# A net of two blocks on one core: subtractions of the fp32r split moved from GpSimd to VectorE, seven casts from VectorE to ScalarE

## The chip, the core and the metric

The kernel runs on one core of one Trainium2 chip, as one launch. The metric is the device time of that launch in microseconds (us). The engines are named as the profile names them: PE (TensorE matmuls), PEld (its weight loads), DVE (VectorE), ACT (ScalarE), POOL (GpSimd) and SP (SyncE, which issues the DMAs).

## What is computed

The reference is a chain of residual layers on 256 tokens of width 1024: a first block of two layers (banded attention with a short convolution, then a gated feed-forward of width 2816) and a second block of two layers (an mLSTM mixer or a stick-breaking mixer, and after it a PEER feed-forward). Cut to the part that the change's largest piece lies in:

```python
def peer_ffn(h, w_q, sub_keys, peer_u, peer_v):
    ...
        s_top, i_top = lax.top_k(s, PEER_TOPK)
    ...
        g_top, pos = lax.top_k(cand, PEER_TOPK)
        expert = jnp.take_along_axis(cand_idx, pos, axis=-1)
        g = jax.nn.softmax(g_top, axis=-1)
        u = jnp.take(peer_u, expert, axis=0)
        act = jax.nn.gelu(jnp.einsum('thkd,td->thk', u, xb).astype(jnp.float32), approximate=False)
        vv = jnp.take(peer_v, expert, axis=0)
        return jnp.einsum('thk,thkd->td', (g * act).astype(xb.dtype), vv)
```

Every sublayer is `x = x + g * norm_or_gate(f(norm(x)))`, so that the next sublayer's first product needs the norm of the whole new row of x.

## The kernel before, in words

The 256 tokens are two tiles of 128 rows (t = 0 and 1). Every weight is streamed from HBM once, as tiles of 128x1024 f32 (`load`, L166, issued by SP). `split_w` makes two fp32r tiles of each: `whi`, a cast (L177, as a rule on ACT), and `wlo` = raw - whi (L180, on DVE or POOL). Activations are split the same way, and `mm3` makes each product as three fp32r matmuls: high by high, high by low, low by high (L185 to L187). Four raw tiles, five `whi` and five `wlo` are held at a time.

**Which engine splits.** A counter `ahead` is set to 0 in `Norm.finish` each time the second row tile's norm is set up. The first four tiles of a stage after that take their engines from two strings (L29): the casts from `FIRST_HI` = "aava" (a is ACT, v is DVE), the subtractions from `FIRST_LO` = "vpvp" (v is DVE, p is POOL). Later tiles are cast on ACT and subtracted on DVE, unless the caller names an engine. The fifth and sixth tile's casts are held behind the norm.

**A transition** is the place between two stages. When the last matmuls of a stage are done, row tile t = 0 is finished first: on DVE the scaled result is made (L300, or L567), x updated (L305, or L568), the sums of squares (ACT, L74) turned into `rstd` (ACT L260, DVE L261), and x times rstd is written to `f` or `xa` by a pair of TENSOR_SCALAR (L91). PE transposes it (`tpx`, L96), ACT and DVE split the transposes into `hhi` and `hlo` (L102 to L106), and the first product of the new stage (`mmA`) can start. The first four weight tiles are split in the same time, on the same engines. There are seven such transitions whose tiles follow the strings; in the first stage of all there is no earlier work to wait for.

**The PEER layers** (`peer`) hold the rest of what the change touches; there are two. For 128 groups of experts, `up(c)` makes a product with 24 matmuls and a gelu. Groups 0 to 63 run beside the routing (top-16 searches on DVE, subtractions on POOL for every third c). After it, for c from 64 to 99, `up` runs beside 32 calls of `weigh`: masks (`e`, L958, L959, L964, on DVE), 16 small matmuls (`pG`, L968) and a multiplication of the activations by the weights (L976, DVE); subtraction on POOL for c % 6 == 1. Then 28 turns of `down(c)` and `up(100 + c)`; then, for c from 28 to 63, `down(c)` with the other 32 calls of `weigh` (below: the weighing stretch); then `down` alone up to 127. `down(c)` casts the activations (`wr`, L988, ACT), subtracts (`wr`, L989: POOL for 28 <= c < 64, else DVE), splits a weight tile (POOL for c % 6 == 1 and c < 64, else DVE) and adds 12 matmuls of 512 columns into four accumulators `acc`.

The program is built by a layer that lists each engine's instructions in the order of a plan, and each engine then runs its list in that order. When an instruction is given to another engine, the lists of all engines can come out in another order.

The lines that the change touches:

```python
29    FIRST_HI, FIRST_LO = "aava", "vpvp"
177   (nc.vector.tensor_copy if FIRST_HI[i:i + 1] == "v" else nc.scalar.copy)(hi, raw)
179   lo_eng = nc.gpsimd if FIRST_LO[i:i + 1] == "p" else nc.vector
180   self.last_lo = lo_eng.tensor_tensor(lo, raw, hi.bitcast(F32), op=ALU.subtract)
```

Of the kernel before, what the change touches and what calls it, by code (L numbers as in the profile page):

```python
# [7 lines left out]
F32 = mybir.dt.float32  # L8
# [5 lines left out]
ALU = mybir.AluOpType  # L14
# [11 lines left out]

WSCALE = 32768.0

FIRST_HI, FIRST_LO = "aava", "vpvp"  # L29

FREE, LAST = 4, 6

# [83 lines left out]
class Net:  # L116
# [776 lines left out]
    def peer(self, l, norm, g2, nxt, out=None):  # L893
        nc, tc, d = self.nc, self.tc, self.d


        N1, NA, FIN, GATE, TAIL = 64, 100, 58, 110, 4
        LAG = 128 - NA
        with ExitStack() as ctx:
# [11 lines left out]
            def up(c, dst, lo_eng=None):  # L911
                w = self.split_w(d["peer_u"][l, c], lo_eng=lo_eng)
                p = self.pa.tile([128, S], F32, tag="sc", name="pA")
                for k in range(KD):
                    mm = self.mm3(p, [v[:, k * 128:(k + 1) * 128] for v in w], [v[:, k, :] for v in h],
                                  k == 0, k == KD - 1)
                return mm, nc.scalar.activation(dst, p, AF.Gelu)  # L917

            def spare(full=False):
                self.calls += 1  # L920
                if self.bg and (self.calls % 2 or full):
                    self.pop()
# [24 lines left out]
            def row(c):  # L947
                c = c % NA
                return act1[:, c, :] if c < N1 else act2[:, c - N1, :]
# [30 lines left out]
            def down(c):  # L980
                if not acc:
                    acc.extend([self.ps.tile([128, 512], F32, tag="mm", name="acc") for _ in range(2)] for _ in range(NT))
                if c < 128 - TAIL // 2:
                    gh, gl = wr[:, 0, c % 2, :], wr[:, 1, c % 2, :]
                else:
                    w2 = C.tile([128, 2, S], F32R, tag="wr2", name="wr2")
                    gh, gl = w2[:, 0], w2[:, 1]
                nc.scalar.copy(gh, row(c))  # L988
                (nc.gpsimd if LAG <= c < 64 else nc.vector).tensor_tensor(gl, row(c), gh.bitcast(F32), op=ALU.subtract)  # L989
                v = self.split_w(d["peer_v"][l, c], lo_eng=nc.gpsimd if c % 6 == 1 and c < 64 else nc.vector)  # L990

                def mm(t, j):
                    ts_ = slice(t * 128, (t + 1) * 128)
                    self.mm3(acc[t][j], (gh[:, ts_], gl[:, ts_]), [y[:, j * 512:(j + 1) * 512] for y in v],
                             c == 0, c == 127)

                if c >= 128 - TAIL:
                    return mm
                for t in range(NT):
                    for j in range(2):  # L1000
                        mm(t, j)

            done = 0
            for c in range(64, NA):
                up(c, row(c), nc.gpsimd if c % 6 == 1 else nc.vector)
                while done < 32 and done * (NA - 65) < (c - 63) * 32:
                    weigh(0, 8 * done)
                    done += 1
            for c in range(LAG):
                down(c)  # L1010
                up(NA + c, row(NA + c), nc.gpsimd if c == 0 else nc.vector)
                spare(True)
            done = 0
            for c in range(LAG, 64):
                down(c)
                while done < 32 and done * (63 - LAG) < (c - LAG + 1) * 32:
                    weigh(1, 8 * done)
                    done += 1
            for c in range(64, 128 - TAIL):
                down(c)  # L1020
                spare(2 * len(self.bg) > GATE - c)
                if c == NA - 1:
                    mid.close()
                    C = P(ctx, "pec", 2)
                if c == GATE:
                    tc.keep_in_program_order(nc.scalar.preload_act_table_set("sqrt_and_others"))
                    if nxt:
                        nxt.prepare()
                    gb = [C.tile([128, 512], F32, tag="g2b", name="g2b") for _ in range(2)]
                    for j in range(2):  # L1030
                        nc.sync.dma_start(gb[j], g2()[:, j * 512:(j + 1) * 512])
# [305 lines left out]
```

## Time and profile before

| | before |
|---|---|
| median of 3 runs (lowest to highest) | 2943.63 us (2941.0 to 2946.9) |
| the profiled execution | 2948.3 us, span 2946.5 us |
| PE, PEld | 2892.2 us (98%), 2600.3 us (88%) |
| DVE | 2176.6 us (74%) |
| ACT | 1424.7 us (48%) |
| POOL | 339.8 us (12%), 176 instructions |
| granted PE clock, mean | 0.987 |
| L180 on DVE, on POOL | 799 and 94 instructions |
| L989 on DVE, on POOL | 184 and 72 instructions |
| L177 on ACT, on DVE | 886 and 7 instructions |

The profile is one execution, 4.7 us above the median of the runs (2948.3 - 2943.63). Its span lies 1.8 us inside its time (2948.3 - 2946.5). An engine's busy share is a mean over stages that have different limits; what a stage is worth is read in the stage. A start in a row is counted from the start of the span; the number in square brackets is how long the engine sat idle before the instruction, and what released it. The granted clock is a share of the full 2.4 GHz.

### The profile page before, as it was taken

What the parts mean: (1) busy time and instruction counts of PE and PEld (TensorE: products, weight loads), DVE (VectorE), ACT (ScalarE), POOL (GpSimd) and SP (SyncE); (2) the same over time, 40 slices, a digit from 0 to 9 for tenths busy, and PEclk for the clock granted to TensorE, in tenths of its full rate; (3) what the DMA queues carried; (4) which work ended last, traced back from release to release, by engine and by line L of the source; (5) the groups of instructions that cost most, each with busy time, mean ns of one, the idle gap of its engine ahead of it and who ended that gap; (6) DMA issues with size and microseconds to landing.
All of it is one profiled execution on the core that took longest, in us unless ns stands there. A gap on an engine that the chain in (4) does not pass through costs nothing.

```text
span 2946.5 us, 50678 instructions
## 1 busy us (share of the span) xinstructions
PE 2892.2 (98%) x19693; PEld 2600.3 (88%) x19693; DVE 2176.6 (74%) x4064; ACT 1424.7 (48%) x2356; POOL 339.8 (12%) x176
## 2 busy tenths in 40 slices
PE   9999999999999999989999999999999999999999
PEld 7898997899897779989999887877899999988887
DVE  6886766886755576978876897686689787459765
ACT  6645445554544554444344334556544434443454
POOL 0001001000100002330100330010023210014100
PEclk9999999999999899999999999999999999999999
DMA  6385775366665444564478458754345545654564
GB/s 220 108 282 185 265 244 184 104 236 231 215 195 171 132 143 152 178 201 145 155 269 281 153 158 276 224 175 129 122 159 180 179 137 158 186 179 139 165 201 146
DMA packets 153572, 542.41 MB, mean 184 GB/s; under 512 B 20003, under 2 KB 21227, under 8 KB 153331
## 3 DMA queue, kind: packets, MB, share of 16 engines
q1 hardware_dynamic: 153330, 539.18, 56.9%
q8 instruction: 154, 2.52, 0.3%
q14 instruction: 88, 0.71, 0.1%
HBM read 538.02 MB, written 1.09 MB: 183 GB/s over the span
## 4 chain that ended last, share of the span: by engine, by line
PE 88%; DVE 10%; DMA 1%; ACT 1%; issue 1%; POOL 0%; SPq 0%; DVEq 0%; ACTq 0%; POOLq 0%
PE acc L185 8%; PE acc L187 8%; PE acc L186 8%; PE mmB L186 7%; PE mmB L187 7%; PE mmB L185 7%; PE pA L185 6%; PE pA L186 6%; PE pA L187 6%; PE mmA L185 5%; PE mmA L186 5%; PE mmA L187 5%; PE pG L968 4%; DVE wlo L180 3%; PE sc L185 1%; DVE whi L177 1%
## 5 line engine op out<-in xcount | busy, mean ns | idle before, releaser
L177 ACT CAST whi<-raw 128x1024 fp32r<-128x1024 f32 x886 | 929.6, 1050 | 822.0 <-PE pA L186 313.7
L180 DVE TENSOR_TENSOR wlo<-raw,whi 128x1024 fp32r<-128x1024 f32 x799 | 988.8, 1241 | 340.8 <-ACT whi L177 337.7
L185 PE MATMUL pA<-hhi,whi 128*128 128x256 f32 x2048 | 586.5, 286 | 10.8 <-ACT act L917 9.8
L186 PE MATMUL pA<-hlo,whi 128*128 128x256 f32 x2048 | 579.9, 283 | 0.0
L187 PE MATMUL pA<-hhi,wlo 128*128 128x256 f32 x2048 | 579.6, 283 | 0.0
L180 POOL TENSOR_TENSOR wlo<-raw,whi 128x1024 fp32r<-128x1024 f32 x94 | 252.6, 2687 | 2143.1 <-ACT whi L177 1897.9
L186 PE MATMUL mmB<-hlo,whi 128*128 128x256 f32 x1480 | 423.2, 286 | 0.0
L187 PE MATMUL mmB<-hhi,wlo 128*128 128x256 f32 x1480 | 421.6, 285 | 0.0
L185 PE MATMUL mmB<-hhi,whi 128*128 128x256 f32 x1480 | 421.5, 285 | 0.0
L185 PEld LDWEIGHTS pA<-hhi,whi 128*128 128x128 f32 x2048 | 394.3, 193 | 15.0 <-ACT act L917 11.4
L185 PE MATMUL acc<-whi,wr 128*128 128x512 f32 x1024 | 405.7, 396 | 0.0
L187 PE MATMUL acc<-whi,wr 128*128 128x512 f32 x1024 | 400.2, 391 | 0.4
L186 PE MATMUL acc<-wlo,wr 128*128 128x512 f32 x1024 | 399.4, 390 | 0.0
L186 PEld LDWEIGHTS pA<-hlo,whi 128*128 128x128 f32 x2048 | 393.2, 192 | 2.2
L187 PEld LDWEIGHTS pA<-hhi,wlo 128*128 128x128 f32 x2048 | 393.0, 192 | 0.0
L988 ACT CAST wr<-act 128x256 fp32r<-128x256 f32 x256 | 103.7, 407 | 405.9 <-PE acc L186 401.0
L186 PEld LDWEIGHTS mmB<-hlo,whi 128*128 128x128 f32 x1480 | 282.9, 191 | 4.3
L187 PEld LDWEIGHTS mmB<-hhi,wlo 128*128 128x128 f32 x1480 | 282.9, 191 | 2.3
L185 PEld LDWEIGHTS mmB<-hhi,whi 128*128 128x128 f32 x1480 | 282.9, 191 | 1.5
L187 PEld LDWEIGHTS acc<-whi,wr 128*128 128x128 f32 x1024 | 192.2, 188 | 45.8 <-DVE wr L989 4.7
L185 PEld LDWEIGHTS acc<-whi,wr 128*128 128x128 f32 x1024 | 193.9, 189 | 35.8
L186 PEld LDWEIGHTS acc<-wlo,wr 128*128 128x128 f32 x1024 | 192.8, 188 | 36.1
(359 smaller groups left out, 4238.2 us busy)
## 6 DMA issues: line engine op xcount, KB each, us to landing
raw<-in_peer_u SPq DMA_DIRECT2D x256, 512.0 KB, 3.7
raw<-in_peer_v SPq DMA_DIRECT2D x256, 512.0 KB, 4.2
adaw<-in_ada_w SPq DMA_DIRECT2D x96, 512.0 KB, 4.6
raw<-in_w_gates SPq DMA_DIRECT2D x80, 512.0 KB, 3.7
raw<-in_w_down SPq DMA_DIRECT2D x44, 512.0 KB, 4.3
raw<-in_w_gate SPq DMA_DIRECT2D x36, 512.0 KB, 4.2
raw<-in_w_up SPq DMA_DIRECT2D x36, 512.0 KB, 3.8
raw<-in_w_qkv SPq DMA_DIRECT2D x24, 512.0 KB, 4.4
```

What stands on the lines that cost most here:

```text
L177: (nc.vector.tensor_copy if FIRST_HI[i:i + 1] == "v" else nc.scalar.copy)(hi, raw)
L180: self.last_lo = lo_eng.tensor_tensor(lo, raw, hi.bitcast(F32), op=ALU.subtract)
L185: nc.tensor.matmul(out, lhsT=lhs[0], rhs=rhs[0], start=start, stop=False)
L186: nc.tensor.matmul(out, lhsT=lhs[0], rhs=rhs[1], start=False, stop=False)
L187: return nc.tensor.matmul(out, lhsT=lhs[1], rhs=rhs[0], start=False, stop=stop)
L968: nc.tensor.matmul(pg[:, :, 4 * g + t], lhsT=e2[:, g, :, t], rhs=e1[:, j, :, t], start=(j == 0), stop=(j == 1))
L988: nc.scalar.copy(gh, row(c))
```

## The change

```diff
-FIRST_HI, FIRST_LO = "aava", "vpvp"
+FIRST_HI, FIRST_LO = "aaaa", "vvvv"
...
                 nc.scalar.copy(gh, row(c))
-                (nc.gpsimd if LAG <= c < 64 else nc.vector).tensor_tensor(gl, row(c), gh.bitcast(F32), op=ALU.subtract)
-                v = self.split_w(d["peer_v"][l, c], lo_eng=nc.gpsimd if c % 6 == 1 and c < 64 else nc.vector)
+                nc.vector.tensor_tensor(gl, row(c), gh.bitcast(F32), op=ALU.subtract)
+                v = self.split_w(d["peer_v"][l, c], lo_eng=nc.vector)
...
             for c in range(64, NA):
-                up(c, row(c), nc.gpsimd if c % 6 == 1 else nc.vector)
+                up(c, row(c), nc.vector)
...
-                up(NA + c, row(NA + c), nc.gpsimd if c == 0 else nc.vector)
+                up(NA + c, row(NA + c), nc.vector)
```

Seven casts go from DVE to ACT. Fifty subtractions of a weight tile go from POOL to DVE: 14 at the seven transitions, and 36 in the two PEER layers (12 in `up` for c from 64 to 99, 2 in `up(100)`, 22 in `down`). All 72 subtractions of activations on POOL go to DVE. The routing's 44 subtractions (c < 64, c % 3 == 0) stay on POOL, with four multiplications and two memsets.

The first place is the first transition that uses the strings, on DVE. `rstd_3279` scales the last result of the old stage, `x_89` is row tile 0 and `x_97` row tile 1, `rstd_3293` is the norm of tile 0.

```order
 L305 SCALAR_TENSOR_TENSOR x_89<-f,rstd_3279,x_89 128x512 x2
-L177 CAST whi<-raw 128x1024
+L180 TENSOR_TENSOR wlo<-raw,whi 128x1024
 L76 TENSOR_SCALAR ss<-ss 128x1
-L180 TENSOR_TENSOR wlo<-raw,whi 128x1024
+L180 TENSOR_TENSOR wlo<-raw,whi 128x1024 x2
 L261 RECIPROCAL rstd_3293<-rstd_3293 128x1
+L300 TENSOR_TENSOR f<-mmA,gb 128x512
 L91 TENSOR_SCALAR f<-x_89,rstd_3293 128x512 x2
-L300 TENSOR_TENSOR f<-mmA,gb 128x512
```

Between the update of x and the norm's pair L91, DVE had a cast and one subtraction; now it has three subtractions and the second row tile's L300.

The second place is the same transition on ACT, where `junk` is the square of x that gives the sum of squares.

```order
 L260 ACTIVATE rstd_3279<-ss_3142 128x1
 L177 CAST whi<-raw 128x1024
-L74 ACTIVATE junk,ss<-x_89 128x512 x2
+L74 ACTIVATE junk,ss<-x_89 128x512
+L177 CAST whi<-raw 128x1024
+L74 ACTIVATE junk,ss<-x_89 128x512
+L177 CAST whi<-raw 128x1024
 L260 ACTIVATE rstd_3293<-ss 128x1
-L177 CAST whi<-raw 128x1024
```

Two casts now stand ahead of the `rstd` of tile 0, one of which was on DVE and one behind it.

The third place is the weighing stretch of the first PEER layer, on DVE. A tile `pG_n` is one call of `weigh`; the product with `wlo_19053` stands right behind the matmuls of `pG_19021` in PE's list, before and after. The first fence is one turn before.

```order
L180 TENSOR_TENSOR wlo_19194<-raw_19191,whi_19193 128x1024 [waits DMAHW7_49,Activation_49]
L976 SCALAR_TENSOR_TENSOR act2_14791<-pG_19021,act2_14791 128x36x8 [waits PE_49]
L976 SCALAR_TENSOR_TENSOR act1_11731<-pG_19021,act1_11731 128x28x8
L964 TENSOR_TENSOR e1_19073<-e0_19070,slots_11727 128x512
L964 TENSOR_TENSOR e1_19083<-e0_19070,slots_11727 128x512
L958 TENSOR_TENSOR e2_19116<-iota4_106,slots_11727 128x1024
L959 TENSOR_TENSOR e0_19164<-iota4_106,slots_11727 128x512 [waits DVE_49]
```

The second is the same turn of the change.

```order
L964 TENSOR_TENSOR e1_19026<-e0_19023,slots_11727 128x512 [waits DVE_49]
L964 TENSOR_TENSOR e1_19036<-e0_19023,slots_11727 128x512
L180 TENSOR_TENSOR wlo_19053<-raw_19050,whi_19052 128x1024 [waits DMAHW4_49]
L976 SCALAR_TENSOR_TENSOR act2_14791<-pG_19021,act2_14791 128x36x8 [waits PE_49]
L976 SCALAR_TENSOR_TENSOR act1_11731<-pG_19021,act1_11731 128x28x8
L958 TENSOR_TENSOR e2_19069<-iota4_106,slots_11727 128x1024
L959 TENSOR_TENSOR e0_19070<-iota4_106,slots_11727 128x512
L989 TENSOR_TENSOR wr_11723<-act1_11731,wr_11723 128x256 [waits Activation_49]
```

Beside the multiplication of `pG_19021`, DVE made the `wlo` that PE needs three turns later; now it makes there the one that PE needs next. The masks `e0` were also made a turn further ahead. The subtraction L989 is new in this list.

## Rows read from the trace of the kernel before

**Rows 1.** The page: engines, the chain that ended last, two groups (busy us, mean ns).

```profile
PE 2892.2 (98%) x19693; PEld 2600.3 (88%) x19693; DVE 2176.6 (74%) x4064; ACT 1424.7 (48%) x2356; POOL 339.8 (12%) x176
...
PE 88%; DVE 10%; DMA 1%; ACT 1%; issue 1%; POOL 0%; SPq 0%; DVEq 0%; ACTq 0%; POOLq 0%
...
L177 ACT CAST whi<-raw 128x1024 fp32r<-128x1024 f32 x886 | 929.6, 1050 | 822.0 <-PE pA L186 313.7
...
L180 POOL TENSOR_TENSOR wlo<-raw,whi 128x1024 fp32r<-128x1024 f32 x94 | 252.6, 2687 | 2143.1 <-ACT whi L177 1897.9
```

**Rows 2.** What PE waited for, whole span: us in total, times, longest us.

```profile
PE tpx L96 <- DVE f L91: 12.2, 6, 2.2
PE tpx L96 <- DVE xa L91: 11.2, 4, 3.9
```

**Rows 3.** Timeline of the first transition, DVE: start us, us, instruction [idle before].

```profile
270.52 2.89 DVE L177 CAST whi<-raw 128x1024 fp32r<-128x1024 f32 x1
...
273.45 1.23 DVE L180 TENSOR_TENSOR wlo<-raw,whi 128x1024 fp32r<-128x1024 f32 x1
...
274.78 2.97 DVE L91 TENSOR_SCALAR f<-x,rstd 128x512 f32<-128x512 f32 x2
277.68 0.68 DVE L300 TENSOR_TENSOR f<-mmA,gb 128x512 f32<-128x512 f32 x1
```

**Rows 4.** The same timeline, POOL.

```profile
270.15 2.71 POOL L180 TENSOR_TENSOR wlo<-raw,whi 128x1024 fp32r<-128x1024 f32 x1 [222.10 <-ACT whi L177]
274.88 2.60 POOL L180 TENSOR_TENSOR wlo<-raw,whi 128x1024 fp32r<-128x1024 f32 x1 [2.02 <-ACT whi L177]
```

**Rows 5.** The same timeline, ACT.

```profile
273.57 0.29 ACT L260 ACTIVATE rstd<-ss 128x1 f32<-128x1 f32 x1 [2.12 <-DVE ss L76]
```

**Rows 6.** The same timeline, PE.

```profile
272.78 0.40 PE L187 MATMUL mmA<-whi,mixlo 128*128 128x512 f32 x1
275.32 0.65 PE L96 MATMUL tpx<-ident,f 128*128 128x128 f32 x4 [2.15 <-DVE f L91]
277.81 0.88 PE L96 MATMUL tpx<-ident,f 128*128 128x128 f32 x4 [1.83 <-DVE f L91]
278.73 0.80 PE L185 MATMUL mmA<-whi,hhi 128*128 128x512 f32 x1
```

**Rows 7.** Timeline of DVE at the second transition, the second row tile's pair.

```profile
479.83 0.88 DVE L91 TENSOR_SCALAR f<-x,rstd 128x512 f32<-128x512 f32 x2
```

**Rows 8.** Windows of 14 us at the seven transitions: busy by engine, PEclk, DMA share, GB/s.

```profile
1945.00:1959.00 14.00, 8.29 (x29) 5.97 (x28) 13.91 (x23) 5.50 (x13) 7.22 (x4) 0.70 0.50 145
2086.00:2100.00 14.00, 10.62 (x51) 8.16 (x51) 13.76 (x26) 7.71 (x20) 4.83 (x2) 1.00 0.40 123
sum 98.00, PE 69.37 PEld 52.06 DVE 93.12 ACT 53.97 POOL 38.17; mean PE 9.91 PEld 7.44 DVE 13.30 ACT 7.71 POOL 5.45
```

**Rows 9.** A window over the weighing stretch of the first PEER layer, same columns.

```profile
1624.00:1780.00 156.00, 155.24 (x1066) 128.53 (x1066) 137.22 (x238) 60.19 (x89) 50.12 (x42) 1.00 0.52 164
```

**Rows 10.** Timeline of the weighing stretch, POOL.

```profile
1643.44 1.03 POOL L989 TENSOR_TENSOR wr<-act,wr 128x256 fp32r<-128x256 f32 x1 [2.93 <-ACT wr L988]
1647.24 0.98 POOL L989 TENSOR_TENSOR wr<-act,wr 128x256 fp32r<-128x256 f32 x1 [2.77 <-ACT wr L988]
...
1652.02 2.41 POOL L180 TENSOR_TENSOR wlo<-raw,whi 128x1024 fp32r<-128x1024 f32 x1
1654.86 0.79 POOL L989 TENSOR_TENSOR wr<-act,wr 128x256 fp32r<-128x256 f32 x1 [0.43 <-ACT wr L988]
1659.07 1.81 POOL L989 TENSOR_TENSOR wr<-act,wr 128x256 fp32r<-128x256 f32 x1 [3.42 <-ACT wr L988]
```

**Rows 11.** Groups of DVE from 1624.5 to 1780 us: count, busy us, mean ns.

```profile
L180 DVE TENSOR_TENSOR wlo<-raw,whi 128x1024 fp32r<-128x1024 f32 x38 | 46.2, 1217 | 8.6 <-ACT whi L177 8.6
L964 DVE TENSOR_TENSOR e<-e,slots 128x512 f16<-128x512 f16 x62 | 36.8, 617 | 1.5 <-PE pG L968 1.1
...
L989 DVE TENSOR_TENSOR wr<-act,wr 128x256 fp32r<-128x256 f32 x6 | 2.5, 421 | 1.6 <-ACT wr L988 1.6
```

**Rows 12.** All of line 964, by form: duration ns min/median/max.

```profile
L964 DVE TENSOR_TENSOR e<-e,slots x256: 403/417/2286, 1331.4 to 2759.2; 128x512 f16<-128x512 f16 x128
```

## The prediction, made before the change was run

> **What bounds the kernel now.** I read the page first, then what PE waited for, then one transition on four engines, then the weighing stretch. PE is busy for 98% of the span and carries 88% of the chain that ended last; DVE carries 10% and POOL 0% [rows 1]. So POOL's own length costs nothing as a sum (the 94 weight subtractions there take 252.6 us, 2.69 us each), and a change that gives DVE more work can gain only where the chain runs through DVE. What PE waited for says where that is: its transposes waited 12.2 us for `f` and 11.2 us for `xa`, both line 91, in ten waits [rows 2]. PE's idle time is there too: the seven windows of 14 us around the transitions hold 98 us, of which PE was busy 69.4, so 28.6 us are idle [rows 8].
>
> The first transition shows why line 91 is late. The pair of TENSOR_SCALAR takes 2.97 us [rows 3], and the same pair takes 0.88 us where POOL has nothing to do [rows 7]. POOL's subtraction started 0.10 us after it and ran 2.60 us [rows 4]; the long part of the pair has the length of that subtraction. The cast on DVE repeats it: 2.89 us from 270.52, beside a POOL subtraction that ran from 270.15 to 272.86. So these two DVE instructions stood still while POOL's subtraction ran, some 2 us each, both in the chain between the update of x and the first transpose. The chain ends with the pair at 277.75, the second four transposes at 277.81 and the first product at 278.73, while the last product of the old stage started at 272.78 [rows 6].
>
> **The transitions, step by step.** The change removes the DVE cast and both POOL subtractions and adds two DVE subtractions, and it puts L300 ahead of the pair. DVE then has, from 270.52 on: three subtractions of 1.23 [rows 3], the two tiny ss and rstd steps (0.15 each, my round figure for what is left between the rows), L300 at 0.68 and the pair at 0.88: 3.69 + 0.30 + 0.68 + 0.88 = 5.55, ending at 276.07 if nothing holds it. ACT is what may hold it. It gets two casts of 1.05 us [rows 1] ahead of its `rstd`, but sat idle for 2.12 us before that [rows 5]: 271.45 + 2.10 = 273.55, which is where its rstd started anyway. The third subtraction cannot start before that cast ends: 273.55 + 1.23 + 0.15 + 0.68 + 0.88 = 276.49. Against 277.75 the pair ends 1.26 to 1.68 us earlier. I take 1.5 for each of the seven, which have the same order of work: **-10.5 us**. The ends: nothing, if the casts wait for tiles that the old stage still reads, or if `hlo` becomes the late one (both updates of the second row tile now stand ahead of it on DVE); and 2.97 - 0.88 = 2.09 for each, -14.6 us in all, if everything that stood still is saved.
>
> The seven casts cost ACT 7 x 1.05 = 7.4 us of an engine that is busy for 48% of the span [rows 1]; beside the idle time just named I count them at nothing. SP's order of loads is not touched.
>
> **Outside the weighing stretch.** In `up` for c from 64 to 99 and in the turns of `down` with `up`, the moved subtractions (14) go onto a DVE that runs beside 24 matmuls of PE for each; a subtraction on DVE costs 1.2, but each on POOL held up a mask L964, which takes 0.42 us at the median and 2.29 at most [rows 12]. That is 1.87 saved against 1.22 spent; I count nothing. If DVE were the bound there, the 14 would cost at most 14 x 1.22 = 17 us, but the chain's 88% of PE speaks against it.
>
> **The weighing stretch** is where the change can lose. One turn takes 3.80 us (wr starts at 1643.44 and 1647.24 [rows 10]), and PE is busy for 155.24 of 156 us [rows 9]. Where a POOL subtraction stands in it, the turn from 1654.86 to 1659.07 takes 4.21, so it lost 0.41; there are three such turns in the first stretch and as many in the second. They go: 6 x 0.4 = **-2.4 us**.
>
> Against that, DVE gets more to do. In the first stretch it was busy for 137.2 us [rows 9]. The 62 masks L964 fall from 36.8 us to 62 x 0.417 = 25.9 [rows 11, 12], since POOL no longer holds them up: -10.9. Six subtractions come, 6 x 1.217 = +7.3, and 36 of the activations at 0.421 = +15.2 [rows 11]. That makes 148.8 of 156, or 95% (it was 88%). DVE's own work still fits, but its order has no lead left: in the second half of the list, some 19 turns, the `wlo` made in a turn is the one that PE needs next, where it was one for three turns later, and the multiplication L976 behind it waits for PE. With no lead every short wait of DVE for PE is handed back to PE. No row shows such a turn. The price is at least 0, because the sum of the work fits, and at most the 0.41 us of the turns in which DVE was late, in all 2 x 36 turns: 29.5 us. I take a third of 0.41, 0.13, for the 19 turns of either layer, nearer to the low end since 7.2 us of a stretch stay free: 2 x 19 x 0.13 = **+5 us**.
>
> The Trainium skill (Perfetto Trace Analysis, Optimizing Scalar/DVE Operations) speaks against the change here: where VectorE is saturated, it says, offloading some work to ScalarE or even GpSimd may make sense. By that sentence the weighing stretch should have kept its subtractions on POOL, and the sum would go with the high end of this term, some 15 us above the time before. The same section adds that GpSimd and VectorE share an SBUF read port, so that moving work between the two might not help; the 2.97 us against 0.88 agree with that.
>
> **Sum.** -10.5 - 2.4 + 5 = -7.9 on the profiled execution's 2948.3: 2940.4 us. That execution is 4.7 above the median of the runs shown, so on the scale of the median 2943.63 - 7.9 = 2935.7; I give **2936**. A measurement of this kernel can tell about 0.2% from no change, 5.9 us, so faster means below 2937.7 and slower above 2949.5.
>
> **The rivals.**
>
> *The gain is half eaten.* ACT's casts or `hlo` come late, so that a transition gains 0.8 instead of 1.5 (-5.6), or the weighing turns cost 0.25 instead of 0.13 (+9.5). Either gives about -3: 2940. For it: the ACT path above leaves no spare time at all (273.55 against 273.57). Against it: a cast late by 0.5 us would move only one subtraction.
>
> *VectorE becomes the bound of the weighing stretch: slower.* DVE has 7.2 us free in a stretch of 36 turns (156 - 148.8), 0.2 us a turn. If its waits for PE take more than that in a turn, each turn is longer than PE's 3.80, and the mechanism decides there. The whole price, 0.41 in all 72 turns, is 29.5, less the 10.5 of the transitions: +19, or 2963; it is slower than before by over 5.9 us from 0.23 us a turn on (10.5 + 5.9 = 16.4, over 72). For it: the missing lead, and L976 right behind `wlo`. Against it: the 88% of before held PE at 99.5% busy, and what held the masks up goes away.
>
> *The clock stays up: faster still.* The windows show a granted clock of 0.70 at the sixth transition and 1.00 at the seventh, where PE was busy for 10.62 us against 9.91 in the mean [rows 8]. 0.70 is a mix of the two levels, 1.2 and 2.4 GHz. The first product after the gap took 0.80 us at the first transition, twice the 0.40 before it [rows 6]. If shorter gaps keep the clock up at half of the seven, each gives back at most 0.30 x 14 = 4.2 us; with about 2 each, -7 more: 2929. Against it: a gap of 4.5 us is still a gap.
>
> *The change does not do what it says.* The order of the lists shows that it does; no chance.
>
> **Chances.** The forecast 0.45, half eaten 0.35, VectorE the bound 0.15, clock 0.05. So faster 0.50 (forecast and clock), same 0.35, slower 0.15. The range goes from 2927 (all of 2.09 us saved at each transition, no price in the weighing stretch: -17, or 2926.6) to 2950, where the slower rival begins with 0.23 us a turn; most of that rival and the luckiest clocks are left out. Where the signs meet, the likeliest case alone runs from 2931 to 2938.
>
> **What would show it.** Right: the pair L91 takes 0.9 us at all seven transitions, POOL shows only 44 weight subtractions, PE's waits for `f` and `xa` fall from 23.4 us to about 13, L964 has no instance above 0.5 us in the weighing stretch, and a turn there takes 3.80 in its first half and about 3.9 in its second. Wrong: PE waits for `hlo` or `wlo` at the transitions as long as it did for L91; or the turns of the weighing stretch go above 4.0 us, with PE waiting for L964 or for `wlo` in each.

## The result, and the profile after

| | before | after |
|---|---|---|
| median (lowest to highest), 5 runs each | 2943.63 us (2941.0 to 2948.44) | 2926.9 us (2918.03 to 2932.55) |
| profiled execution, its span | 2948.3, 2946.5 us | 2919.5, 2917.7 us |
| granted PE clock, mean | 0.987 | 0.994 |

The ratio is 0.9933, with a 95% interval from 0.9913 to 0.9954: 16.7 us faster by the medians. The profiled execution of the changed kernel lies 7.4 us under its median, that of before 4.7 over, so the two profiles differ by 28.8 us; some of that is the difference between executions, and the runs further down tell how much. One run of those further down (FREE = 1, 5631.74 us) counts as slow and is left out of its ratio.

The page of the changed kernel, the lines that answer to [rows 1], and POOL's groups of instructions (busy us, mean ns, then the idle time before them):

```profile
PE 2878.2 (99%) x19693; PEld 2589.4 (89%) x19693; DVE 2163.6 (74%) x4179; ACT 1433.5 (49%) x2363; POOL 145.3 (5%) x54
...
PE 89%; DVE 8%; ACT 1%; DMA 1%; issue 1%; SPq 0%; DVEq 0%; ACTq 0%
```

```profile
L180 POOL TENSOR_TENSOR wlo<-raw,whi 128x1024 fp32r<-128x1024 f32 x44 | 128.8, 2927 | 797.0 <-ACT whi L177 788.9 <-PE pA L187 8.1
```

PE's busy time fell from 2892.2 to 2878.2 us with the same 19693 matmuls, so 14.0 of the 28.8 us are shorter matmuls and 14.8 are idle time. DVE took over 50 + 72 subtractions (50 x 1.24 + 72 x 0.42 = 92 us) and gave up seven casts of 2.4 us, and yet it is busy for 13 us less than before: the time in which POOL held it up had been counted as busy. PE waited for less (answers to [rows 2]; us in total, times, longest):

```profile
PE tpx L96 <- DVE f L91: 7.5, 4, 2.5
...
PE tpx L96 <- DVE xa L91: 3.9, 3, 2.0
PE mmA L186 <- DVE wlo L180: 2.8, 3, 1.6
PE tpx L96 <- issue: 2.5, 1, 2.5
```

The waits for `f` and `xa` fell from 23.4 to 11.4 us; 2.5 more of the same kind lie under "issue". New is 2.8 us for `wlo`.

The first transition, DVE (answers to [rows 3]) and PE (to [rows 6]); start us, us, instruction:

```profile
271.42 1.22 DVE L180 TENSOR_TENSOR wlo<-raw,whi 128x1024 fp32r<-128x1024 f32 x1
...
272.62 1.22 DVE L180 TENSOR_TENSOR wlo<-raw,whi 128x1024 fp32r<-128x1024 f32 x1
274.14 1.23 DVE L180 TENSOR_TENSOR wlo<-raw,whi 128x1024 fp32r<-128x1024 f32 x1 [0.30 <-ACT whi L177]
...
275.35 0.67 DVE L300 TENSOR_TENSOR f<-mmA,gb 128x512 f32<-128x512 f32 x1
275.94 0.87 DVE L91 TENSOR_SCALAR f<-x,rstd 128x512 f32<-128x512 f32 x2
```

```profile
273.68 0.40 PE L187 MATMUL mmA<-whi,mixlo 128*128 128x512 f32 x1
276.47 1.97 PE L96 MATMUL tpx<-ident,f 128*128 128x128 f32 x8 [2.39 <-DVE f L91]
278.48 0.80 PE L185 MATMUL mmA<-whi,hhi 128*128 128x512 f32 x1
```

The order is the one that the lists showed: three subtractions, L300, the pair, which takes 0.87 instead of 2.97 us. The third subtraction waited 0.30 us for ACT's cast, as worked out. From the start of the old stage's last product to that of the new stage's first it is 278.48 - 273.68 = 4.80 us, where it was 278.73 - 272.78 = 5.95. At all seven transitions the first row tile's pair takes 0.87 or 0.88 us. The second row tile's still takes 1.67 us at the first, beside a multiplication left on POOL (L286, 2.81 us from 281.53), and 2.12 at the sixth, beside POOL's memsets (L771, 3.56 us from 1925.81).

The windows of 14 us at the seven transitions, of the changed kernel (answers to [rows 8]: busy by engine, then the granted clock):

```profile
269.00:283.00 14.00, 11.15 (x46) 8.32 (x45) 11.99 (x24) 10.04 (x26) 1.47 (x1) 0.88 0.48 162
467.00:481.00 14.00, 11.16 (x55) 8.38 (x54) 12.11 (x34) 10.32 (x29) 0.00 (x0) 1.00 0.55 175
734.00:748.00 14.00, 11.17 (x55) 8.41 (x54) 12.05 (x32) 10.61 (x29) 3.75 (x1) 1.00 0.53 188
928.00:942.00 14.00, 11.41 (x57) 8.74 (x56) 13.58 (x35) 9.99 (x29) 0.00 (x0) 1.00 0.51 166
1063.00:1077.00 14.00, 11.65 (x53) 9.20 (x52) 12.28 (x28) 10.29 (x25) 0.00 (x0) 0.88 0.48 150
1921.00:1935.00 14.00, 10.87 (x52) 8.31 (x51) 13.87 (x31) 9.45 (x24) 3.56 (x2) 1.00 0.47 148
2060.00:2074.00 14.00, 12.19 (x62) 9.19 (x61) 12.98 (x29) 9.05 (x25) 0.00 (x0) 1.00 0.44 135
sum 98.00, PE 79.60 PEld 60.56 DVE 88.86 ACT 69.77 POOL 8.78; mean PE 11.37 PEld 8.65 DVE 12.69 ACT 9.97 POOL 1.25
```

And the five windows of the kernel before that did not stand among the rows:

```profile
269.00:283.00 14.00, 9.99 (x39) 7.36 (x39) 12.98 (x23) 8.80 (x24) 5.31 (x2) 0.88 0.49 151
467.00:481.00 14.00, 10.03 (x37) 7.45 (x36) 12.78 (x27) 8.08 (x23) 4.80 (x2) 0.76 0.43 134
736.00:750.00 14.00, 10.45 (x38) 7.72 (x37) 12.98 (x24) 8.38 (x22) 5.30 (x2) 0.76 0.50 149
933.00:947.00 14.00, 10.08 (x37) 7.63 (x36) 13.52 (x23) 7.66 (x20) 5.11 (x2) 0.76 0.35 111
1075.00:1089.00 14.00, 9.91 (x44) 7.77 (x43) 13.21 (x20) 7.84 (x17) 5.60 (x2) 0.88 0.37 113
```

Two things changed in them. PE's idle time fell from 98 - 69.37 = 28.6 to 98 - 79.60 = 18.4 us, so by 10.2. And the granted clock, which was below 1.00 in six of the seven windows (1.26 in all, times 14 us: 17.6 us), is below it in two (0.24, or 3.4 us). The second is what the prediction left out of its sum.

Not all of the low clock stands at transitions. In the profile of before, span x (1 - granted clock), the loss if PE's clock set all of the time, is 38.9 us, of which these windows hold 17.6. Another 15.4 lie in one stretch between the fourth and the fifth transition, the small products of the mLSTM mixer (L705 to L720): there the granted clock is 0.50 from 1005 to 1036 us, although PE is busy all that time. The changed kernel has the same stretch (13.7 us), and the gaps at the transitions do not reach it.

The weighing stretch: the window (answers to [rows 9]), the groups on DVE from 1603.5 to 1759 us ([rows 11]) and all of L964 ([rows 12]).

```profile
1603.00:1759.00 156.00, 155.44 (x1054) 127.39 (x1053) 140.69 (x279) 62.33 (x88) 0.00 (x0) 1.00 0.48 156
```

```profile
L180 DVE TENSOR_TENSOR wlo<-raw,whi 128x1024 fp32r<-128x1024 f32 x44 | 53.5, 1220 | 5.5 <-ACT whi L177 5.5
...
L964 DVE TENSOR_TENSOR e<-e,slots 128x512 f16<-128x512 f16 x62 | 23.7, 419 | 0.8 <-PE pG L968 0.8
...
L989 DVE TENSOR_TENSOR wr<-act,wr 128x256 fp32r<-128x256 f32 x42 | 17.6, 420 | 3.0 <-ACT wr L988 2.9
```

```profile
L964 DVE TENSOR_TENSOR e<-e,slots x256: 409/419/427, 1309.1 to 2732.3; 128x512 f16<-128x512 f16 x128
```

The moved work is there (six more L180, 36 more L989), no mask takes more than 0.43 us any more, and PE is as busy as it was (155.44 against 155.24 us). DVE is busy for 140.7 us where I expected 148.8.

### The profile page after: what moved, and what is told of

Read it like the earlier page. It is cut to its first block, busy times and chain, and to the rows that moved or that the text cites. A ratio compares the mean times of both kernels' runs of the same rounds, so it can differ in the third digit from the quotient of the medians.

```text
span 2917.7 us, 50501 instructions
## 1 busy us (share of the span) xinstructions
PE 2878.2 (99%) x19693; PEld 2589.4 (89%) x19693; DVE 2163.6 (74%) x4179; ACT 1433.5 (49%) x2363; POOL 145.3 (5%) x54
## 4 chain that ended last, share of the span: by engine, by line
PE 89%; DVE 8%; ACT 1%; DMA 1%; issue 1%; SPq 0%; DVEq 0%; ACTq 0%
PE acc L185 8%; PE acc L187 8%; PE acc L186 8%; PE mmB L186 7%; PE mmB L187 7%; PE mmB L185 7%; PE pA L185 6%; PE pA L186 6%; PE pA L187 6%; PE mmA L186 5%; PE mmA L187 5%; PE mmA L185 5%; PE pG L968 4%; DVE wlo L180 2%; PE sc L185 1%
## 5 line engine op out<-in xcount | busy, mean ns | idle before, releaser
L180 DVE TENSOR_TENSOR wlo<-raw,whi 128x1024 fp32r<-128x1024 f32 x849 | 1048.7, 1240 | 336.5 <-ACT whi L177 332.9
L187 PE MATMUL acc<-whi,wr 128*128 128x512 f32 x1024 | 400.4, 391 | 2.6 <-DVE wr L989 2.4
L185 PE MATMUL acc<-whi,wr 128*128 128x512 f32 x1024 | 393.2, 396 | 0.0
L537 DVE CUSTOM_DVE_ANT_0 adaw<-adaw,cb 128x1024 f32<-128x1024 f32 x112 | 136.9, 1223 | 86.4 <-DMA adaw<-in_ada_w 77.5
```

The source lines that it names most:

```text
L185: nc.tensor.matmul(out, lhsT=lhs[0], rhs=rhs[0], start=start, stop=False)
L187: return nc.tensor.matmul(out, lhsT=lhs[1], rhs=rhs[0], start=False, stop=stop)
L537: nc.vector.tensor_tensor_reduce(w, w, self.csilu, 1.0, 0.0, op0=ALU.mult, op1=ALU.add, accum_out=col[:, j:j + 1])
```

## The experiments

Two questions were put: which part of the change carries the gain, and how much of it is the shorter gap itself and how much the clock. The *clock theory*: the gaps at the transitions shrink by what the prediction worked out, and beyond that the clock is kept up. The *PEER theory*: taking POOL out of the PEER layers carries a good part. For the first part there was a second pair: the *lock theory* (POOL's subtractions hold DVE up) against the *cast theory* (a cast on DVE is the cost).

**The two strings alone.**

```diff
-FIRST_HI, FIRST_LO = "aava", "vpvp"
+FIRST_HI, FIRST_LO = "aaaa", "vvvv"
```

> Only the two strings (transitions); the PEER layers keep POOL. Clock theory: the seven gaps shrink by about 11 us in all, and the granted clock rises from 0.987 to 0.990 or more, so that the time falls by 12 to 18 us (ratio 0.994 to 0.996). PEER theory: a gain of 4 to 8 us and the rest of the change's gain missing.

Measured: 2925.89 us, ratio 0.9939 [0.9916, 0.9963], beside 2942.84 before: 17 us faster. This is the whole gain of the change.

**The four edits in the PEER layers alone**, the strings as before.

```diff
-                (nc.gpsimd if LAG <= c < 64 else nc.vector).tensor_tensor(gl, row(c), gh.bitcast(F32), op=ALU.subtract)
-                v = self.split_w(d["peer_v"][l, c], lo_eng=nc.gpsimd if c % 6 == 1 and c < 64 else nc.vector)
+                nc.vector.tensor_tensor(gl, row(c), gh.bitcast(F32), op=ALU.subtract)
+                v = self.split_w(d["peer_v"][l, c], lo_eng=nc.vector)
...
-                up(c, row(c), nc.gpsimd if c % 6 == 1 else nc.vector)
+                up(c, row(c), nc.vector)
...
-                up(NA + c, row(NA + c), nc.gpsimd if c == 0 else nc.vector)
+                up(NA + c, row(NA + c), nc.vector)
```

> Only the four edits in the PEER layers; the strings as before. Clock theory: -3 to +5 us, with PE's waits for f and xa and the granted clock as before (about 23 us, 0.987). PEER theory: 6 to 12 us faster, among it a shorter wait of PE in the routing (5.3 us before, 1.9 after).

Measured: 2944.43 us, ratio 0.9997 [0.9982, 1.0013]: no difference. PE's waits for `f` and `xa` are those of before (12.3 and 11.5 us). The PEER theory falls: 108 of the 122 moved subtractions change nothing that can be measured.

**The seven casts alone, and the 14 subtractions alone.**

```diff
-FIRST_HI, FIRST_LO = "aava", "vpvp"
+FIRST_HI, FIRST_LO = "aaaa", "vpvp"
```

> Strings aaaa and vpvp: the seven casts go to ACT, POOL keeps its 14 subtractions at the transitions, all else as before. If POOL's subtractions are what held DVE (the lock theory), the pair L91 still takes about 3 us and little is gained: 0 to 4 us. If the cast on DVE was the cost, over 8 us are gained. PE's waits for f and xa: 18 to 24 us by the first, under 13 by the second.

```diff
-FIRST_HI, FIRST_LO = "aava", "vpvp"
+FIRST_HI, FIRST_LO = "aava", "vvvv"
```

> Strings aava and vvvv: the cast of the third tile stays on DVE, alone there and so near 0.7 us, POOL has no subtraction at a transition. Lock theory: the pair L91 takes 0.9 us everywhere and most of the gain is there, 10 to 17 us. Cast theory: under 5 us.

Measured: the casts alone 2943.67 us, ratio 0.9996 [0.9981, 1.0011]; the subtractions alone 2928.13 us, 0.9941 [0.9921, 0.9961]. The first transition with the casts alone, DVE and then POOL:

```profile
272.91 2.28 DVE L180 TENSOR_TENSOR wlo<-raw,whi 128x1024 fp32r<-128x1024 f32 x1 [0.79 <-ACT whi L177]
...
275.29 2.77 DVE L91 TENSOR_SCALAR f<-x,rstd 128x512 f32<-128x512 f32 x2
```

```profile
271.38 2.72 POOL L180 TENSOR_TENSOR wlo<-raw,whi 128x1024 fp32r<-128x1024 f32 x1 [222.06 <-ACT whi L177]
274.51 2.88 POOL L180 TENSOR_TENSOR wlo<-raw,whi 128x1024 fp32r<-128x1024 f32 x1 [0.41 <-ACT whi L177]
```

With the subtractions alone, DVE at the same place:

```profile
273.85 0.68 DVE L177 CAST whi<-raw 128x1024 fp32r<-128x1024 f32 x1
...
276.90 0.88 DVE L91 TENSOR_SCALAR f<-x,rstd 128x512 f32<-128x512 f32 x2
```

This is the lock theory's result on both sides. The cast that took 2.89 us beside POOL takes 0.68 on the same engine without it, and the pair 0.88; with POOL still there the pair keeps its 2.77 us, and even a DVE subtraction that overlaps POOL's takes 2.28 instead of 1.22. The Trainium skill (SBUF — State Buffer, SBUF: two separate sides) has the mechanism: GpSimd and VectorE share a pair of ports, and for VectorE instructions in a two-port mode or with two SBUF inputs, whichever engine starts first holds the pair for its whole instruction, while the other blocks. These rows agree with it (2.28 and 2.77 us beside POOL, 1.22 and 0.88 without). Not all went as expected: the waits of PE for `f` and `xa` were 26.7 us with the casts alone, more than before, and with the subtractions alone one L91 of `xa` still took 2.1 us, beside the memsets that stay on POOL (L771, 3.89 us from 1930.33).

**The gap widened again.** On the changed kernel, the normed row is multiplied by 1.0 before it is transposed (PAD = 2, and with PAD = 1 half as often); nothing else differs.

```diff
+PAD = 2
...
             nc.vector.tensor_scalar(buf[:, s], src[:, s], self.r[t], ROOT, op0=ALU.mult, op1=ALU.mult)
+        for i in range(2 * PAD if t == 0 and net.gate is not None else 0):
+            s = slice(i % 2 * 512, (i % 2 + 1) * 512)
+            nc.vector.tensor_scalar(buf[:, s], buf[:, s], 1.0, None, op0=ALU.mult)
```

> The changed kernel, with four more multiplications by 1.0 of the normed row (1.76 us of DVE) ahead of the first transposes of each transition: the gaps are about as long as before the change, all else is as after it. Clock theory: the time rises by more than 8 x 1.76 = 14 us over the changed kernel, to about 2945 or above, and low-clock stretches stand behind several gaps again. If gap length alone counts: +14 us or less and the clock stays at 0.991 to 0.994.

> The changed kernel with half of the earlier padding: 0.88 us of DVE ahead of the first transposes, eight times, 7.0 us in all. If gap and clock go together in steps, the granted clock lies between those of the changed kernel and of the full padding (0.9920 and 0.9897 in the mean) and the time between 2930 and 2937. If the clock needs a gap as long as before's, the clock stays at 0.992 and the time is 2930 to 2934.

Measured: PAD = 2 2940.09 us, ratio 0.9984 [0.9970, 0.9998]; PAD = 1 2931.38 us, 0.9962 [0.9949, 0.9975]. The second transition with PAD = 2, a window, DVE and PE, and PE at the same place of the changed kernel (the lines of the padded kernel are numbered up to four higher):

```profile
467.00:483.00 16.00, 11.06 (x45) 8.69 (x44) 13.62 (x34) 9.35 (x23) 0.00 (x0) 0.79 0.37 117
```

```profile
474.18 1.42 DVE L95 TENSOR_SCALAR f<-f 128x512 f32<-128x512 f32 x4
```

```profile
471.07 0.40 PE L191 MATMUL mmA<-whi,flo 128*128 128x512 f32 x1
475.42 1.12 PE L100 MATMUL tpx<-ident,f 128*128 128x128 f32 x8 [3.94 <-DVE f L95]
477.53 0.80 PE L189 MATMUL mmA<-whi,hhi 128*128 128x512 f32 x1 [0.99 <-ACT hhi L106]
478.12 0.63 PE L190 MATMUL mmA<-wlo,hhi 128*128 128x512 f32 x1
```

```profile
468.72 0.40 PE L187 MATMUL mmA<-whi,flo 128*128 128x512 f32 x1
471.66 1.06 PE L96 MATMUL tpx<-ident,f 128*128 128x128 f32 x8 [2.55 <-DVE f L91]
472.96 0.50 PE L185 MATMUL mmA<-whi,hhi 128*128 128x512 f32 x1 [0.24 <-ACT hhi L102]
473.30 0.40 PE L186 MATMUL mmA<-wlo,hhi 128*128 128x512 f32 x1
```

The four multiplications cost 1.42 us as a row, and some 1.34 beside the row ahead of them, so the eight places add about 10.7 us of DVE, not the 14 that I had written. The time rose by 13.2 us over the first runs of the changed kernel (15.1 over the second, below), more than what was added but short of the 2945 that I had given to the clock theory. The rows show the clock's part: after a gap of 4.24 us the second product takes 0.40 us, after one of 6.46 us 0.63. The widened gap brings the low clock back behind it (0.79 in the window, 1.00 in that of the changed kernel), and the products after it run at the lower of the two levels, 1.2 against 2.4 GHz. PAD = 1 lies between, in time (2931.38) and in clock (0.9907 in the mean), as the steps of gap and clock together had it.

**What the clock costs.** Each run lists its span and granted clock, so every run can be split into span x (1 - clock) and the rest. Means over all runs of a kernel:

| kernel | runs | time us | granted clock | span x (1 - clock) us | span x clock us |
|---|---|---|---|---|---|
| before | 84 | 2944.3 | 0.9888 | 32.9 | 2909.6 |
| changed | 11 | 2925.8 | 0.9921 | 23.1 | 2900.9 |
| strings alone | 6 | 2925.9 | 0.9928 | 21.0 | 2903.2 |
| subtractions alone | 6 | 2927.1 | 0.9928 | 21.0 | 2904.3 |
| PEER layers alone | 12 | 2943.9 | 0.9887 | 33.4 | 2908.8 |
| casts alone | 12 | 2943.6 | 0.9893 | 31.4 | 2910.4 |
| changed, PAD = 1 | 9 | 2932.4 | 0.9907 | 27.4 | 2903.2 |
| changed, PAD = 2 | 12 | 2939.9 | 0.9897 | 30.4 | 2907.7 |

Among the 84 runs of the kernel before, where the program does not differ, a straight line gives 0.92 us of span for each us of span x (1 - clock); among the 11 of the changed kernel 0.98. If that held between two kernels as well, the change would have gained 8.7 us at an equal clock and 9.8 us through the clock, and PAD = 2 would give 6.8 and 7.3 of them back. The traces check it. In the two profiles shown, span x (1 - clock) fell by 21.8 us and PE's busy time by 14.0; in the second pair of profiles by 21.7 and 16.8 (2897.0 to 2880.2). So a us of it stands for 0.64 to 0.77 us of longer matmuls, and the clock's part of the 18.5 us in the means is about 6 to 10, the rest shorter gaps. Around the seven transitions alone, from the same matmul to the same matmul, the first pair of profiles differs by 21.2 us: 10.5 of idle time and 10.8 of longer matmuls. So the two parts are about equal; which is the larger is not shown.

**Both kernels again**, unchanged.

> The kernel before, unchanged: ratio 1.000, within 0.2%. If the 5.3 us wait of PE in the first routing and the low clock behind it belong to the kernel before, they show again; if they were of that one execution, they do not. Times over all its runs should fall with the granted clock.

> The changed kernel once more: 2920 to 2932, ratio 0.993 to 0.996. Clock theory: over its runs the span falls by 0.8 to 1.0 us for each us of span x (1 - granted clock), its mean granted clock is 0.991 to 0.994 where the kernel before has 0.989. If the routing's short wait (1.9 us) was of one execution, it differs here.

Measured: 2943.26 us, ratio 1.0006 [0.9992, 1.0020], and 2924.95 us, ratio 0.9940 [0.9924, 0.9957]. The 5.3 us for which PE waited for the gelu (L917) in the first routing before did not come back (2.0 us at most in the second profile of that kernel), and the second profile of the changed kernel has one of 4.5 us, where its first had 1.9: this wait comes and goes in both kernels and is no part of the gain. The second profile of the changed kernel has low clock behind the second transition too (0.88 in the window from 467 to 481 us, where the first had 1.00): which gaps lose the clock differs between executions of one program. The stretch of small products in the mLSTM mixer differs more: over the profiles its span x (1 - clock) goes from 3.4 us (the PEER layers alone, FREE = 2) to 17.1 (PAD = 1, FREE = 1), and the same 295 matmuls of PE, the 6600th to the 6895th, take 67.2 to 79.6 us. No change here touches it, so it is spread, and a large part of it.

**The activations' subtractions back on POOL.**

```diff
-                nc.vector.tensor_tensor(gl, row(c), gh.bitcast(F32), op=ALU.subtract)
+                (nc.gpsimd if LAG <= c < 64 else nc.vector).tensor_tensor(gl, row(c), gh.bitcast(F32), op=ALU.subtract)
```

> The changed kernel with the 72 subtractions of activations (L989, c from 28 to 63) back on POOL. If the weighing stretch loses through DVE's load, as the prediction has it, this gains 2 to 7 us over the changed kernel: 2920 to 2925. If DVE's work there lies beside PE's, no difference: 2925 to 2929.

Measured: 2924.0 us, ratio 0.9931 [0.9918, 0.9945], beside 0.9940 [0.9924, 0.9957] for the changed kernel on the same chip: no difference that shows. The time lies in the first of the two ranges, 0.95 us under the changed kernel's, so the run does not decide between them. From the same matmul to the same matmul, the two weighing stretches take 155.2 and 154.8 us in its profile, against 156.7 and 155.5 in the changed kernel's (156.5 and 155.6 in its second), so a gain of 1 to 2 us may lie there.

**Fewer tiles ahead of the norm.** FREE says how many of a stage's first weight tiles are split without being held behind the norm; it was 4 in both kernels.

```diff
-FREE, LAST = 4, 6
+FREE, LAST = 2, 6
```

> The changed kernel with the third and fourth tile's casts also held behind the norm (FREE = 2): two subtractions of 1.2 us leave the path ahead of L91. If DVE's subtractions now set the gap, it shrinks by 1.5 to 2.5 us at each transition, the clock stays up more often (0.994 or more) and the time falls by another 8 to 18 us, to 2909 to 2919. Rival: PE then waits for wlo of these tiles in the first products as long as it waited for L91: 2924 to 2930.

> The same with FREE = 1: three subtractions leave the path. If L91 is all that matters, another 3 to 8 us below free2. Rival: the second tile's wlo is late for the first products, so that PE waits for it: same as free2 or 2 to 6 us above.

> The changed kernel with only the fourth tile's cast also held behind the norm (FREE = 3). One subtraction of 1.2 us leaves the path ahead of L91, and the tile that PE needs last is the one that comes late. If it is the best of both: 2916 to 2923. If PE pays for it in the first products, as with FREE = 2: 2925 to 2930.

Measured: FREE = 2 2928.78 us, 0.9942 [0.9925, 0.9960]; FREE = 1 2951.05 us, 1.0025 [1.0012, 1.0039]; FREE = 3 2920.93 us, 0.9917 [0.9898, 0.9935]. What PE waited for, with FREE = 2 and then with FREE = 3:

```profile
PE tpx L96 <- DVE f L91: 11.5, 4, 4.0
...
PE mmA L185 <- ACT whi L177: 3.4, 2, 2.0
```

```profile
PE tpx L96 <- DVE xa L91: 6.8, 4, 2.8
...
PE tpx L96 <- DVE f L91: 3.2, 5, 1.5
```

Taking two subtractions off the path did not shorten the waits: with FREE = 2 PE waits 11.5 us for `f`, more than the 7.5 of the changed kernel, and for casts besides. The rival was right there, and FREE = 1 is worse than it had it. FREE = 3 has the lowest time of all and beats the kernel before by 0.83%; against the changed kernel on the same chip (0.9940) its interval overlaps, so that it is better is likely, not shown.

## Why the prediction was wrong

It gave 2936 with a range from 2927 to 2950; measured were 2926.9, just outside at the lower end, and the gain was twice the 7.9 us of the sum.

- **The transitions at an equal clock: right.** The forecast was 1.5 us for each, 10.5 in all; PE's idle time in the seven windows fell by 10.2 us. At the first it is 5.95 to 4.80 us from product to product; that is 1.15, just under the 1.26 to 1.68 worked out, and the `wlo` waited for ACT as foreseen. The mechanism, POOL's subtraction holding up the cast and the pair, is shown by the runs with either half of the strings.
- **The clock: the step that failed.** The sum has no term for it. The rival named it, with 0.05 and 7 us, against it that "a gap of 4.5 us is still a gap". The runs show some 6 to 10 us through the clock, about as much as the gaps themselves gave. The windows to see it were in the trace of before: 0.88, 0.76, 0.76, 0.76, 0.88, 0.70 and 1.00. I looked at two of them, and summed on an execution's time as if its low clock stayed. Half of their 17.6 us as a term would have put the forecast near 2927; that half is hindsight, as no row of before says how much comes back.
- **The weighing stretch: right that it fits, wrong in the price.** The forecast was +5 for the lost lead and -2.4 for the held-up turns; the PEER edits together measured 0.9997 [0.9982, 1.0013], or -0.9 us (from -5.3 to +3.8), which holds both the +2.6 and zero. From the same matmul to the same matmul the first stretch takes 156.1 and 156.4 us in the two profiles of before, 156.7 and 156.5 in those of the changed kernel, and the second 156.0 and 156.0, then 155.5 and 155.6. So both terms came out near nothing. That -2.4 is too much stood in [rows 9]: PE was idle for 0.76 us of the whole stretch (156 - 155.24), less than three turns of 0.41. DVE's load came out at 140.7 and not 148.8 us; the masks L958, which POOL also held up (23.2 us before, 20.5 after), had not been counted, nor the overlap between neighbours. So the slower rival, built on that load, had no ground.
- **The casts on ACT at nothing: right** (0.9996). **The half eaten gain:** some of it happened, as 2.8 us of waits for `wlo` in the first products, inside the term's range.
- **The Trainium skill's sentence on offloading from a saturated VectorE** (Perfetto Trace Analysis, Optimizing Scalar/DVE Operations) was taken to put the time some 15 us higher. No run shows a loss of that size: the PEER edits alone cost at most 3.8 us by their interval, and with the activations back on POOL the time is the same within the spread.

## What to carry to other kernels

A GpSimd instruction that is itself on no chain can lengthen the chain, when VectorE's instructions beside it stand still: look for instances of one VectorE form that take three times its median, and what GpSimd does at that moment. Then move only those off GpSimd; 14 subtractions carried this change, and 108 others did nothing. Where gaps of PE shrink, read the granted clock of the windows around them before and count what it may give back as a term of the sum, with its spread from run to run, not as a rival. Read it over the rest of the span too: here 15.4 us of it stood away from the gaps, and shorter gaps do not give those back.

## What the runs showed of the hardware

The pair of f32 TENSOR_SCALAR of 128x512 took 0.88 us alone and 2.97 beside a GpSimd subtraction; a cast of 128x1024 0.68 and 2.89; a two-input subtraction 1.22 and 2.28. Executions of one program differ in the granted clock (0.986 to 0.990 in twelve runs of the kernel before) and in time with it, by 0.92 us for each us of span x (1 - clock); that accounts for most of the spread of its times. The granted clock was also 0.50 for some 30 us in which PE was busy throughout with small products (before, 1005 to 1036 us), where one of them (L713, 64x256) took 1.22 us for a pair and 0.70 ahead of it. Why one execution keeps the clock through a gap, or through those products, and the next does not is left open. A test with PE kept at work inside a gap of the old length, which would show the clock's share without a change of the gap, was not tried.
